# The third layer's modulation in a two-stage transformer kernel: scale and shift summed behind a bar, the gate formed on the tensor engine behind the experts

## The chip, the cores and the metric

The kernel runs on one core of one Trainium2 chip. The metric is the device time of one execution in microseconds (us); smaller is better. A core has a tensor engine (PE, with PEld for its weight loads), a vector engine (DVE), a scalar engine (ACT), GpSimd (POOL) and a sync engine (SP). Each takes its own instructions, and engines wait for each other by semaphores. Here SP's queue starts nearly all large transfers.

## The reference

Two blocks of two layers each work on 256 rows of width 1024 in f32. Each of the four layers has a mixer and a feed-forward part, and each part has a scale, a shift and a gate that come from a vector `c`:

```
def modulation(c, w, b):                       # first block; w is 1024 x 3072
    m = jnp.einsum("bd,de->be", jax.nn.silu(c), w) + b
    shift, scale, gate = jnp.split(m, 3, axis=-1)
...
# first block, layer 1 (the second of the four), feed-forward part
    logits = jnp.einsum("btd,de->bte", h, w_router).astype(jnp.float32)
    top_v, top_i = lax.top_k(logits, TOP_K)    # 2 of 8 experts for each row
...
# second block, layer 0 (the third of the four)
        mod = (cond @ w_mod[l] + b_mod[l])[:, None, :]
        sh_a, sc_a, g_a, sh_f, sc_f, g_f = jnp.split(mod, N_MOD, axis=-1)
        h = rms_norm_2(x, norm_mix[l]) * (1 + sc_a) + sh_a
...
        x = x + g_a * (jnp.concatenate([o_m, o_d], axis=-1) @ w_out[l])
```

## The kernel before

The work goes through eight steps: mixer and feed-forward part of each of four layers. Step 3 is the second layer's mixer, step 4 the router with eight experts, step 5 the attention of the third layer. Weights come in tiles of 1 MB into a pool `raw` of four buffers (two more, `rawx`, during the experts). Each is split by `split` into `hi` (a cast on ACT, line 159) and `lo` (a subtraction on DVE, line 160), and a product of f32 precision is three matmuls of these parts (lines 178 to 180; line 654 in the output projections).

A part's modulation is a product of a vector with a 1024x1024 block of weights. There are two ways to make it. `mod_rows` has DVE scale each of eight groups of 128 weight rows by its element of silu(c) and add it to an accumulator `macc` of 128x1024 (lines 318 and 320, two for each tile of 1 MB); `mod_done` then sums over the partitions on PE: eight products with one column each for a scale or a shift (`col`), two products of 128x512 for a gate. `mod_gate_pe` has PE do the whole: products of 128x512 with silu(c), broadcast to 128 columns, as the stationary part and the weight tile as the moving one, in plain f32, 16 for a gate and two more for its bias.

Which modulations are made beside which step is a table, `plan`. Before, step 4 begins with all three of the third layer's mixer, key (2, 0): scale, shift and gate by `mod_rows`. `LAG[4]` = 30 lowers their priority for the scheduler that puts each engine's instructions in order, and `self.bar` is None, so that they may also stand ahead of the end of step 3. `bar` is otherwise the last instruction of a norm's inverse root (line 220), and `behind` and `issue_after` keep work behind it.

The router part of step 4: `make_hf` transposes the normalised x of the second layer (`xn`) on PE, eight pairs through PSUM buffers of the pool `pp` (two buffers), and writes hf with scale and shift applied, on ACT and DVE in turn (lines 507 and 508). `route` multiplies by the router's weights (16 small products), copies the logits (line 1071) and forms the choice in small DVE steps (to line 1098, the selection `sel` at line 1082); a count goes to a register, and a branch on it follows. Then the experts run, and their results are gathered in four PSUM accumulators `ysum`. `resid_rms` makes the residual and two norms of it (lines 602 to 616), for which `two_rows` loads the gain and the shift of the post-norm into a `raw` buffer (line 479). Step 5 begins with the transposes of that result.

Of the kernel before, what the change touches and what calls it, by code (L numbers as in the profile page):

```python
# [14 lines left out]
ACT = mybir.ActivationFunctionType  # L15
ALU = mybir.AluOpType
# [4 lines left out]
KD = 8  # L21
# [46 lines left out]
class _Net:  # L68
# [210 lines left out]
    def mod_gate_pe(self, key):  # L279

        nc = self.nc
        w, b, j, c0 = self.mod_src(key)
        if self.modpos == 0:
            self.modacc = self.tl("gate", [128, D])
            nc.gpsimd.dma_start(out=self.modacc[0:1, :], in_=b[j * D:(j + 1) * D].unsqueeze(0))
        g = self.modacc
        h, k0 = self.modpos // 4, self.modpos % 4 * 2
        hs = slice(h * 512, (h + 1) * 512)
        if k0 == 0:
            self.modps = self.ps(pool="pa")  # L290
            self.mm(self.modps, self.ones[0:1, :], g[0:1, hs], True, False)
        wv = w.rearrange("(k p) n -> p k n", p=128)
        v = self.raw(wv[:, k0:k0 + 4, j * D + h * 512:j * D + (h + 1) * 512])
        for i in range(4):
            c = self.csil[:, c0 + k0 + i:c0 + k0 + i + 1]
            self.mm(self.modps, c.to_broadcast([128, 128]), v[:, i], False, k0 + i == KD - 1)
        if k0 == 4:
            self.plus(key, g[:, hs], self.modps)

    def mod_rows(self, key):  # L300

        nc = self.nc
        V = nc.vector
        w, b, j, c0 = self.mod_src(key)
        row = key[2] == "gate"
        if self.modpos == 0:
            self.modacc = self.tl("macc", [128, D])
            if row:
                nc.gpsimd.memset(self.modacc, 0.0)
                nc.gpsimd.dma_start(out=self.modacc[0:1, :], in_=b[j * D:(j + 1) * D].unsqueeze(0))  # L310
        acc = self.modacc
        wv = w.rearrange("(k p) n -> p k n", p=128)
        v = self.raw(wv[:, self.modpos:self.modpos + 2, j * D:(j + 1) * D])
        for i in range(2):
            k = self.modpos + i
            c = self.csil[:, c0 + k:c0 + k + 1]
            if k == 0 and not row:
                V.tensor_scalar(acc, v[:, i], c, None, ALU.mult)
            else:
                V.scalar_tensor_tensor(acc, v[:, i], c, acc, ALU.mult, ALU.add)  # L320

    def mod_done(self, key):

# [172 lines left out]
    def make_hf(self, xn, A, B):  # L496

        S, V = self.nc.scalar, self.nc.vector
        f = self.tl("h", [128, KD, T], tag="hh")
        for q in range(4):  # L500
            p = self.ps((128, 2, T))
            for t in range(2):
                for j in range(2):
                    k = 2 * q + j
                    self.tr(p[:, j, t * 128:(t + 1) * 128], xn[:, t, k * 128:(k + 1) * 128])
            k = 2 * q
            S.activation(f[:, k], p[:, 0], ACT.Identity, bias=B[:, k:k + 1], scale=A[:, k:k + 1])
            V.tensor_scalar(f[:, k + 1], p[:, 1], A[:, k + 1:k + 2], B[:, k + 1:k + 2], ALU.mult, ALU.add)
        return f

    def make_h(self, xn, A, B):
# [549 lines left out]
    def route(self, xn, hf):  # L1061
        nc, a = self.nc, self.a
        S, V, G = nc.scalar, nc.vector, nc.gpsimd
        wr = self.sc([128, KD, NE])
        G.dma_start(out=wr, in_=a["moe_router"][0].rearrange("(k p) e -> p k e", p=128))
        p = self.ps()
# [1 line left out]
            for k in range(KD):  # L1068
                self.mm(p[:, t * 8:t * 8 + 8], hf[:, k, t * 128:(t + 1) * 128], wr[:, k], k == 0, k == KD - 1)
        L = self.sc([128, 2, NE])  # L1070
        V.tensor_copy(L, p[:, 0:16].rearrange("p (t e) -> p t e", t=2))
        La = L[:, :, :, None].to_broadcast([128, 2, NE, NE])
        Lb = L[:, :, None, :].to_broadcast([128, 2, NE, NE])
        gt, eq = self.sc([128, 2, NE, NE]), self.sc([128, 2, NE, NE])
# [17 lines left out]
        p = self.ps()  # L1092
# [17 lines left out]
        p = self.ps()  # L1110
# [390 lines left out]
    def run(self):  # L1501
# [9 lines left out]
        SC, SH, GA = "scale", "shift", "gate"  # L1511
# [2 lines left out]
            1: [(0, 0, GA), (0, 1, SC), (0, 1, SH)],  # L1514
            2: [(0, 1, GA), (1, 0, SC), (1, 0, SH), (1, 0, GA), (1, 1, SC), (1, 1, SH)],
            3: [(1, 1, GA)],
            4: [(2, 0, SC), (2, 0, SH), (2, 0, GA)],
            5: [(2, 1, SC), (2, 1, SH)],
            6: [(2, 1, GA), (3, 0, SC), (3, 0, SH), (3, 0, GA), (3, 1, SC), (3, 1, SH)],
            8: [(3, 1, GA)],  # L1520
        }
        self.gates_pe = {(0, 0, GA)}
        LAG = {1: 100, 3: 100, 4: 30, 5: 30}
        FILL = {1: (4, 1, 1, 3, 1, 2), 2: (3, 2, 2), 3: (1, 1, 1, 1, 0, 0), 6: (2, 3), 8: (1, 0)}
        self.mods, self.modq, self.modpos = {}, [], 0
# [11 lines left out]
        for s in range(1, 9):  # L1537
            l, i = (s - 1) // 2, (s - 1) % 2
            self.step = s
            one = s < 5  # L1540
            if s == 2:
                self.later.append(self.rope_setup)
            with self.phase(**SIZES[s]):
                if one:
                    A, B = self.ab(l, i, g, b)
                else:
                    A, B = self.ab(l, i, self.c1("norm_ffn_2" if i else "norm_mix_2", l - 2))
                if s == 4:
                    self.bar = None
                    with self.phase(**ROUTE):  # L1550
                        self.mod_start(plan[4], LAG[4])
                        self.fill(KD * KD)
                        hf = self.make_hf(xn, A, B)
                        st = self.route(xn, hf)
                    with self.phase(**EXP):
                        order = self.granules()
                        ready = [self.raw(src) for src in order[:5]]
                        ready = [self.split(v) for v in ready[:2]] + ready[2:] + [self.raw(order[5])]
                        self.moe_over(st, A, B)
                        ysum = st[4]  # L1560
                        self.experts(0, *st[:4], A, B, ysum, order, True, ready)
                    get = lambda t, hh: ysum[t][hh]
                else:
                    h = self.make_h(xn, A, B)
                    self.mod_start(plan.get(s, []), LAG.get(s, 0))
                    if i == 0:
                        get = self.mixer(l, h, FILL[s]) if one else self.attn2(l - 2, h)
                    elif one:
                        get = self.ffn(h, a["ffn_w1"][0], a["ffn_w3"][0], a["ffn_w2"][0], FILL[s])
                    else:  # L1570
                        get = self.ffn(h, a["w_gate_2"][l - 2], a["w_up_2"][l - 2], a["w_down_2"][l - 2], FILL[s])
                rows = (a["post_ln_g"][l, i], a["post_ln_b"][l, i]) if one else None
                if s == 4:
                    x, xn = self.resid_rms(get, x, self.mod(l, i, "gate"), self.two_rows(*rows))
                else:
                    x, xn = self.resid(get, x, self.mod(l, i, "gate"), one, s < 8)
                if s < 4:
                    g, b = self.c1("post_ln_g", s - 1), self.c1("post_ln_b", s - 1)
                    x = xn
                    self.later.append(lambda x=x, r=rows: self.affine(x, *r))  # L1580
# [35 lines left out]
```

## Time and profile before

| what | value |
|---|---|
| median of 3 runs | 2067.67 us (2066.92 to 2073.77) |
| the profiled execution, its own time | 2068.1 us |
| its span in the trace | 2066.0 us |
| PE busy | 1926.2 us (93%) |
| DVE busy | 1643.8 us (80%) |
| ACT busy | 1208.2 us (58%) |
| HBM read | 552.19 MB |

Times within the trace count from the start of the span. A line of a profile names the source line, the engine, the operation, what it writes and reads (`out<-in`) and, in brackets, how long the engine had been idle before it and what let it go.

### The profile page before, as it was taken

To read this page: it belongs to the slowest core of one execution; us is meant where nothing else is said; L and a number is where in the kernel's file an instruction comes from. 1 tells how busy PE (TensorE), PEld (TensorE's weight loads), DVE (VectorE), ACT (ScalarE), POOL (GpSimd) and SP (SyncE) were. 2 spreads that over 40 slices of the span, in tenths; PEclk is the share of its full clock that TensorE was granted. 3 is DMA by queue.
4 is the path that set the end of the run, shared out by engine and by line. 5 is a ranking of instruction groups with operands and counts; after the bars stand their busy time and mean duration, and the time that the engine had idled before them with its cause. 6 is when DMAs were issued, how large, how long until landed. Compare 5 with 4: busy or idle time off the path is not lost.

```text
span 2066.0 us, 29939 instructions
## 1 busy us (share of the span) xinstructions
PE 1926.2 (93%) x11481; PEld 1660.4 (80%) x11481; DVE 1643.8 (80%) x2412; ACT 1208.2 (58%) x1817; POOL 50.2 (2%) x100
## 2 busy tenths in 40 slices
PE   3998999898499999999999999969989999998999
PEld 3887999886378787878778888858869998978998
DVE  6888987898598888888888888889778887667554
ACT  3455445562488767767776777755554546555442
POOL 4000000100000000000000000000000000000000
PEclk9999999998699999999999999979999999999999
DMA  9576999665399999899999999958339995326662
GB/s 325 184 276 214 348 329 316 195 223 205 144 330 362 339 332 341 319 357 346 345 326 350 348 355 358 364 187 279 138 119 349 335 328 164 123 86 220 204 204 82
DMA packets 283238, 555.25 MB, mean 269 GB/s; under 512 B 10172, under 2 KB 137520, under 8 KB 283088
## 3 DMA queue, kind: packets, MB, share of 16 engines
q1 hardware_dynamic: 280000, 549.49, 75.1%
q0 software_dynamic: 2656, 3.20, 0.9%
q8 instruction: 91, 1.49, 0.3%
q10 hardware_dynamic: 432, 0.58, 0.1%
q14 instruction: 59, 0.48, 0.1%
HBM read 552.19 MB, written 1.05 MB: 268 GB/s over the span
## 4 chain that ended last, share of the span: by engine, by line
PE 63%; DVE 6%; ACT 2%; issue 2%; DMA 0%; ACTq 0%; DVEq 0%
PE pp L179 11%; PE pp L180 11%; PE pp L178 11%; PE pa L654 6%; PE ya L179 4%; PE ya L178 4%; PE ya L180 4%; PE pp L187 3%; DVE lo L160 2%; PE pj L178 2%; PE pj L179 1%; PE pj L180 1%; PE sa L183 1%; PE pp L183 1%; ACT hi L159 1%
## 5 line engine op out<-in xcount | busy, mean ns | idle before, releaser
L160 DVE TENSOR_TENSOR lo<-raw,hi 128x1024 fp32r<-128x1024 f32 x660 | 786.0, 1219 | 177.3 <-ACT hi L159 168.6
L159 ACT CAST hi<-raw 128x1024 fp32r<-128x1024 f32 x660 | 667.4, 1050 | 344.2 <-PE pp L179 141.8
L178 PE MATMUL pp<-h,hi 128*128 128x256 f32 x960 | 270.7, 282 | 0.0
L180 PE MATMUL pp<-h,lo 128*128 128x256 f32 x960 | 267.8, 279 | 0.0
L179 PE MATMUL pp<-h,hi 128*128 128x256 f32 x960 | 267.7, 279 | 0.0
L160 DVE TENSOR_TENSOR lo<-rawx,hi 128x1024 fp32r<-128x1024 f32 x176 | 208.3, 1219 | 40.2 <-ACT hi L159 38.9
L320 DVE SCALAR_TENSOR_TENSOR macc<-raw,const,macc 128x1024 f32<-128x1024 f32 x168 | 215.2, 1281 | 9.9 <-DMA raw<-in_w_mod_dram 7.1
L180 PEld LDWEIGHTS pp<-h,lo 128*128 128x128 f32 x960 | 182.2, 190 | 0.1
L159 ACT CAST hi<-rawx 128x1024 fp32r<-128x1024 f32 x176 | 176.9, 1050 | 9.2 <-PE pp L180 7.4
L179 PEld LDWEIGHTS pp<-h,hi 128*128 128x128 f32 x960 | 180.6, 188 | 1.7 <-issue 1.2
L178 PEld LDWEIGHTS pp<-h,hi 128*128 128x128 f32 x960 | 180.3, 188 | 1.7 <-ACT hi L159 1.0
L179 PE MATMUL pp<-lo,h 128*128 128x512 f32 (+1 forms) x480 | 174.9, 365 | 1.3 <-DVE lo L160 1.0
L178 PE MATMUL pj<-hi,h 128*128 128x256 f32 x576 | 168.3, 293 | 7.2 <-ACT h L530 4.0
L178 PE MATMUL pp<-hi,h 128*128 128x512 f32 (+1 forms) x480 | 173.5, 362 | 0.2 <-ACT f L528 0.2
L179 PE MATMUL pj<-lo,h 128*128 128x256 f32 x576 | 165.1, 288 | 1.8 <-DVE lo L160 1.8
L180 PE MATMUL pj<-hi,h 128*128 128x256 f32 x576 | 164.8, 288 | 0.0
L654 PE MATMUL pa<-hi,s 128*128 128x512 f32 x528 | 148.2, 390 | 0.0
L179 PE MATMUL pp<-lo,xe 128*128 128x512 f32 (+1 forms) x384 | 144.9, 377 | 1.2 <-DVE lo L160 1.0
L180 PE MATMUL pp<-hi,x 128*128 128x512 f32 (+1 forms) x384 | 143.7, 374 | 0.0
L178 PE MATMUL pp<-hi,xe 128*128 128x512 f32 (+1 forms) x384 | 143.6, 374 | 0.0
L180 PE MATMUL pp<-hi,xe 128*128 128x512 f32 (+1 forms) x384 | 143.1, 373 | 0.0
L179 PE MATMUL ya<-lo,s 128*128 128x512 f32 x352 | 140.8, 400 | 0.0
(474 smaller groups left out, 3518.5 us busy)
## 6 DMA issues: line engine op xcount, KB each, us to landing
raw<-in_moe_w_dram SPq DMA_DIRECT2D x176, 1024.0 KB, 6.3
rawx<-in_moe_w_dram SPq DMA_DIRECT2D x88, 1024.0 KB, 6.3
raw<-in_ada_w_dram SPq DMA_DIRECT2D x48, 1024.0 KB, 6.7
raw<-in_w_mod_dram SPq DMA_DIRECT2D x48, 1024.0 KB, 6.9
raw<-in_w_in_dram SPq DMA_DIRECT2D x42, 1024.0 KB, 6.0
raw<-in_ffn_w_dram SPq DMA_DIRECT2D x33, 1024.0 KB, 6.3
raw<-in_w_gate_dram SPq DMA_DIRECT2D x22, 1024.0 KB, 5.2
raw<-in_w_up_dram SPq DMA_DIRECT2D x22, 1024.0 KB, 5.3
```

Source lines behind the costliest of these rows:

```text
L159: self.nc.scalar.copy(h, v[:, z:z + m])
L160: self.nc.vector.tensor_tensor(l, v[:, z:z + m], h.bitcast(F32), ALU.subtract)
L178: mm(out, lhsT=a[0], rhs=b[0], start=start, stop=False)
L179: mm(out, lhsT=a[0], rhs=b[1], start=False, stop=False)
L180: mm(out, lhsT=a[1], rhs=b[0], start=False, stop=stop)
L183: self.nc.tensor.matmul(out, lhsT=lhsT, rhs=rhs, start=start, stop=stop)
L187: self.nc.tensor.transpose(out, in_, self.ident[:p, :p])
L320: V.scalar_tensor_tensor(acc, v[:, i], c, acc, ALU.mult, ALU.add)
L654: mm(accs[t][h], lhsT=y[ia][:, s], rhs=W[ib][:, h * 512:(h + 1) * 512], start=start and ia == 0 and ib == 0, stop=stop and ia == 1)
```

## The change

The third layer's gate leaves the table's entry of step 4 and is made by `mod_gate_pe` after the experts, into a buffer of `pp`. Scale and shift lose their lag and are put behind `bar`, the end of the second mixer's norm. The logits' copy is put behind the last of their sums. `make_hf` writes all of hf on ACT.

```
@@ mod_gate_pe
-            self.modps = self.ps(pool="pa")
+            self.modps = self.ps(pool=self.gps)
@@ mod_rows
-                V.scalar_tensor_tensor(acc, v[:, i], c, acc, ALU.mult, ALU.add)
+                self.mod_last = V.scalar_tensor_tensor(acc, v[:, i], c, acc, ALU.mult, ALU.add)
@@ make_hf
-            V.tensor_scalar(f[:, k + 1], p[:, 1], A[:, k + 1:k + 2], B[:, k + 1:k + 2], ALU.mult, ALU.add)
+            S.activation(f[:, k + 1], p[:, 1], ACT.Identity, bias=B[:, k + 1:k + 2], scale=A[:, k + 1:k + 2])
@@ route
-        V.tensor_copy(L, p[:, 0:16].rearrange("p (t e) -> p t e", t=2))
+        with self.tc.issue_after(self.mod_last.ins):
+            V.tensor_copy(L, p[:, 0:16].rearrange("p (t e) -> p t e", t=2))
@@ run
-            4: [(2, 0, SC), (2, 0, SH), (2, 0, GA)],
+            4: [(2, 0, SC), (2, 0, SH)],
-        self.gates_pe = {(0, 0, GA)}
+        self.gates_pe = {(0, 0, GA), (2, 0, GA)}
+        self.gps = "pa"
-                    self.bar = None
                     with self.phase(**ROUTE):
-                        self.mod_start(plan[4], LAG[4])
-                        self.fill(KD * KD)
+                        self.mod_start(plan[4])
+                        with self.tc.issue_after(self.bar):
+                            self.fill(KD * KD)
+                        self.bar = None
                         hf = self.make_hf(xn, A, B)
                         st = self.route(xn, hf)
...
                     get = lambda t, hh: ysum[t][hh]
+
+                    self.gps = "pp"
+                    self.mod_start([(2, 0, GA)])
+                    self.fill(KD)
+                    self.gps = "pa"
```

On PE, between the last product of the second mixer and the first of the router, this stood before (`pp_5437` and `pp_5465` are the column sums of scale and shift, `pp_5495` and `pp_5498` the gate's two products, `x_5327` is xn, `pp_5532` the logits):

```order
L183 MATMUL pp_5437<-const_115,macc_5419 128x1 x8
L183 MATMUL pp_5465<-const_115,macc_5447 128x1 x8
...
L183 MATMUL pa_5583<-const_276 128x512
L183 MATMUL pp_5495<-macc_5475,const_115 128x512
L183 MATMUL pp_5498<-macc_5475,const_115 128x512
L187 MATMUL pp_5502<-const_113,x_5327 128x128 x4
L187 MATMUL pp_5509<-const_113,x_5327 128x128 x4
L187 MATMUL pp_5516<-const_113,x_5327 128x128 x4
L187 MATMUL pp_5523<-const_113,x_5327 128x128 x4
L183 MATMUL pp_5532<-sh_5530,h_5501 128x8 x16
```

And now:

```order
L183 MATMUL pa_5557<-const_276 128x512
L183 MATMUL pp_5437<-const_115,macc_5419 128x1 x8
L183 MATMUL pp_5465<-const_115,macc_5447 128x1 x8
L187 MATMUL pp_5476<-const_113,x_5327 128x128 x4
L187 MATMUL pp_5483<-const_113,x_5327 128x128 x4
L187 MATMUL pp_5490<-const_113,x_5327 128x128 x4
L187 MATMUL pp_5497<-const_113,x_5327 128x128 x4
L183 MATMUL pp_5506<-sh_5504,h_5475 128x8 x16
```

The gate's two products are gone, and the column sums of scale and shift stand directly ahead of the transposes.

On DVE, from the accumulators' end to the steps of the choice, this stood before (`macc_5475` is the gate's accumulator, `t_5549` the logits, `lo` the low parts of expert weights):

```order
L320 SCALAR_TENSOR_TENSOR macc_5475<-raw_5490,const_121,macc_5475 128x1024
L160 TENSOR_TENSOR lo_5628<-raw_5613,hi_5627 128x1024
...
L160 TENSOR_TENSOR lo_9694<-raw_5617,hi_9693 128x1024
L508 TENSOR_SCALAR h_5501<-pp_5502,col_5405,col_5407 128x256
L508 TENSOR_SCALAR h_5501<-pp_5509,col_5405,col_5407 128x256
L508 TENSOR_SCALAR h_5501<-pp_5516,col_5405,col_5407 128x256
L508 TENSOR_SCALAR h_5501<-pp_5523,col_5405,col_5407 128x256
L1071 COPY t_5549<-pp_5532 128x16
L1075 TENSOR_TENSOR sh_5551<-t_5549 128x128
L1076 TENSOR_TENSOR sh_5552<-t_5549 128x128
L1078 TENSOR_TENSOR sh_5552<-sh_5552,const_113 128x128
```

And now (`macc_5447` is the shift's accumulator, `t_5523` the logits):

```order
L320 SCALAR_TENSOR_TENSOR macc_5447<-raw_5460,const_121,macc_5447 128x1024 x2
L353 SCALAR_TENSOR_TENSOR col_5464<-pp_5465,const_272 128x8
L541 TENSOR_TENSOR col_16831<-col_5436,const_264 128x8
L160 TENSOR_TENSOR lo_5598<-raw_5587,hi_5597 128x1024
L160 TENSOR_TENSOR lo_5602<-raw_5587,hi_5601 128x1024
L1072 COPY t_5523<-pp_5506 128x16
L1076 TENSOR_TENSOR sh_5525<-t_5523 128x128
L1077 TENSOR_TENSOR sh_5526<-t_5523 128x128
L160 TENSOR_TENSOR lo_5606<-raw_5589,hi_5605 128x1024
L1079 TENSOR_TENSOR sh_5526<-sh_5526,const_113 128x128
L160 TENSOR_TENSOR lo_5610<-raw_5589,hi_5609 128x1024
L1080 TENSOR_TENSOR sh_5525<-sh_5525,sh_5526 128x128
```

All 16 sums of scale and shift now stand behind the inverse root's last step and end in the first row shown; two of the six splits stand ahead of the logits' copy and four between the steps behind it.

On SP's queue, at the end of the experts, the rows of the post-norm were followed by the attention's weights (`in_w_in`), and had directly behind them the last expert's weights:

```order
L131 DMA raw_16679<-in_moe_w_dram 128x2x1024
L479 DMA raw_16720<-in_post_ln_g_dram 128x1024
L479 DMA raw_16720<-in_post_ln_b_dram 128x1024
L131 DMA raw_16918<-in_w_in_dram 128x8x256
L131 DMA raw_16981<-in_w_in_dram 128x8x256
```

And now:

```order
L131 DMA raw_16653<-in_moe_w_dram 128x2x1024
L131 DMA raw_16698<-in_w_mod_dram 128x4x512
L131 DMA raw_16704<-in_w_mod_dram 128x4x512
L131 DMA raw_16713<-in_w_mod_dram 128x4x512
L131 DMA raw_16719<-in_w_mod_dram 128x4x512
L479 DMA raw_16726<-in_post_ln_g_dram 128x1024
L479 DMA raw_16726<-in_post_ln_b_dram 128x1024
L131 DMA raw_16924<-in_w_in_dram 128x8x256
L131 DMA raw_16987<-in_w_in_dram 128x8x256
```

The gate's four tiles stand between the last expert's weights and the rows of the post-norm, in the same four buffers.

## Rows read from the trace of the kernel before

**Rows 1.** Page, 40 slices of 51.65 us: PE's busy tenths and its granted clock.
```profile
PE   3998999898499999999999999969989999998999
PEclk9999999998699999999999999979999999999999
```

**Rows 2.** Timeline of PE around the router (start, duration, line, operation, idle before).
```profile
512.82 3.62 PE L183 MATMUL pp<-const,macc 128*128 128x1 f32 x32
...
531.72 3.55 PE L183 MATMUL pp<-macc,const 128*128 128x512 f32 x4 [14.39 <-DVE macc L320]
535.11 0.60 PE L187 MATMUL pp<-const,x 128*128 128x128 f32 x4
...
539.70 5.15 PE L183 MATMUL pp<-sh,h 128*128 128x8 f32 x32 [0.78 <-DVE h L508]
```

**Rows 3.** Stretches: length, busy PE, PEld, DVE, ACT, POOL, clock, DMA share, GB/s.
```profile
463.00:473.00 10.00, 6.35 (x22) 4.80 (x22) 6.78 (x13) 4.02 (x11) 0.00 (x0) 0.68 0.52 182
...
478.30:490.00 11.70, 10.49 (x43) 7.70 (x44) 8.66 (x32) 5.17 (x15) 0.90 (x1) 0.62 0.26 86
490.00:513.00 23.00, 23.00 (x108) 18.99 (x106) 19.66 (x29) 4.45 (x7) 0.00 (x0) 1.00 0.84 320
...
518.00:532.00 14.00, 0.28 (x1) 0.31 (x2) 13.93 (x15) 7.95 (x7) 0.00 (x0) 0.50 0.63 225
```

**Rows 4.** Timeline of ACT, at the router and behind the experts.
```profile
523.23 1.24 ACT L582 ACTIVATE x<-x,t,t 128x1024 f32<-128x1024 f32 x1 [25.64 <-DVE t L581]
...
538.50 1.02 ACT L507 ACTIVATE h<-pp,col,col 128x256 f32<-128x256 f32 x2 [1.29 <-PE pp L187]
...
1378.96 1.06 ACT L612 ACTIVATE x<-x 128x1024 f32<-128x1024 f32 x1
```

**Rows 5.** Timeline of DVE around the router.
```profile
523.04 0.15 DVE L581 SCALAR_TENSOR_TENSOR t<-t,t 128x1 f32<-128x1 f32 x1
523.16 3.93 DVE L320 SCALAR_TENSOR_TENSOR macc<-raw,const,macc 128x1024 f32<-128x1024 f32 x3
527.00 2.28 DVE L1103 TENSOR_TENSOR h<-x,x 128x2048 fp32r<-128x2048 f32 x1
...
531.54 5.76 DVE L160 TENSOR_TENSOR lo<-raw,hi 128x1024 fp32r<-128x1024 f32 x5
...
544.88 0.17 DVE L1071 COPY t<-pp 128x16 f32<-128x16 f32 x1 [4.78 <-PE pp L183]
...
546.59 0.17 DVE L1082 TENSOR_SCALAR t<-t 128x16 f32<-128x16 f32 x1
```

**Rows 6.** Waits from 463 to 565: who for whom, total us, times, longest.
```profile
PE pa L187 <- DVE P L943: 6.7, 2, 4.2
```

**Rows 7.** Timeline of DVE in the second mixer's softmax.
```profile
473.45 1.27 DVE L320 SCALAR_TENSOR_TENSOR macc<-raw,const,macc 128x1024 f32<-128x1024 f32 x1
```

**Rows 8.** Timeline of PE behind the experts.
```profile
1363.35 2.24 PE L183 MATMUL pa<-s,s 128*128 128x512 f32 x8 [0.33 <-ACT s L1261]
...
1383.73 1.97 PE L187 MATMUL pp<-const,x 128*128 128x128 f32 x8 [12.37 <-DVE x L615]
```

**Rows 9.** Groups by line and form: count, busy us, mean ns of one, idle before.
```profile
L159 ACT CAST hi<-raw 128x1024 fp32r<-128x1024 f32 x660 | 667.4, 1050 | 344.2 <-PE pp L179 141.8
...
L183 PE MATMUL pa<-raw,const 128*128 128x512 f32 x32 | 15.1, 601 | 0.0
...
L318 DVE TENSOR_SCALAR macc<-raw,const 128x1024 f32<-128x1024 f32 x16 | 12.0, 752 | 2.6 <-DMA raw<-in_ada_w_dram 1.4 <-DMA raw<-in_w_mod_dram 0.7 <-PE pa L183 0.4
```

**Rows 10.** Transfers issued from 1340 to 1400: count, KB each, median us to landing.
```profile
raw<-in_w_in_dram SPq DMA_DIRECT2D x5, 1024.0 KB, 5.2
...
raw<-in_post_ln_g_dram SPq DMA_DIRECT2D x1, 512.0 KB, 4.8
raw<-in_post_ln_b_dram SPq DMA_DIRECT2D x1, 512.0 KB, 6.6
```

**Rows 11.** Timeline of DVE in the norm behind the experts.
```profile
1372.19 1.27 DVE L608 SCALAR_TENSOR_TENSOR x<-x,t,raw 128x1024 f32<-128x1024 f32 x1
```

## The prediction

> **What bounds the kernel now.** I read the slices of the page first: TensorE (PE) is busy in nine tenths or more of most of them, with two holes, in the 11th and the 27th slice of 51.65 us, where the granted clock sinks too [rows 1]. Those two holes are the router and the seam between the experts and the third layer, and the change touches both. So I read each of them instruction by instruction.
>
> The router's hole: PE ends the column sums of the next layer at 516.4 (512.82 + 3.62) [rows 2], stands still in the stretch 518 to 532 at a clock of 0.50 [rows 3], and is let go at 531.72 by VectorE (DVE), after an idle of 14.39 us, for the two products that sum the gate's accumulator. Only behind them, at 535.11, come the transposes of xn [rows 2], although ScalarE (ACT) had the second half of xn ready at 523.23 + 1.24 = 524.5 [rows 4]. DVE has no gap there: up to 537.3 it does the steps of the inverse root, the eight sums of the gate, the low part of xn and six weight splits [rows 5]. DVE's queue sets the router's start, and PE's order hands it on: what waits first holds what stands behind.
>
> The mixer's end, before that: from 490 to 513 PE is busy all the time at full clock; between 463 and 490 it is not [rows 3], and 6.7 us of that, in two waits, is put down to DVE's probabilities P [rows 6]. In front of the second wait stand two sums of the third layer's scale, between DVE's maxima; one is shown [rows 7].
>
> The seam: PE's wait of 12.37 us up to 1383.73 is for the normalised x [rows 8], a pure chain of DVE and ACT. PE is free there, DVE and ACT are not.
>
> **The change part by part.** All times are on the clock of the profiled execution.
>
> *Sums that leave the mixer.* All 16 sums of scale and shift were done in or beside the mixer; now they wait for the bar, the last step of the inverse root. The two of [rows 7] stood in the chain of maxima, each for 1.2 us; without them P comes later only by ACT's exponentials, which I put at 1.5 us earlier than now. The lower bound of this is nothing, the upper the 6.7 us of [rows 6]. I take 1.5, because on both sides of 463 to 490 PE has no gap that DVE could close [rows 3].
>
> *Sums behind the bar.* Eight gate sums leave this place and 16 others come. The inverse root is no longer broken up: its result came at 523.04 with four sums between its steps, at 1.31 each (3.93 for three) [rows 5], so without them at 517.8, say 518.1 as the steps' own latency then shows. From there: 14 sums at 1.31 (18.3), two opening products at 0.75 (1.5) [rows 9], the low part of xn, 2.28 [rows 5]: 540.2. In between stands the first column, which DVE reads from eight products of PE with one column each. Sixteen such took 3.62 us [rows 2] at full clock, so eight take 1.8, and 3.6 if twice as slow; the router's 16 products in two levels took 5.15 [rows 2], so I take 2.7. DVE has one sum (1.3) to cover it and waits 1.4: 541.6. Less the mixer's 1.5: 540.1. Transfers are no bound: the second four tiles can each be issued when DVE has done with one of the first four, and a tile of 1 MB lands in 5.2 us [rows 10], before DVE comes to it.
>
> *The transposes behind the columns.* In PE's new order both column sums stand ahead of the transposes of xn, where before the gate's products did. So the transposes begin at 540.1 + 2.7 = 542.8 instead of 535.11: 7.7 later. This is what PE's order costs. The Trainium skill, "TensorE: Matmul & The Clock Gate", section "Step-by-step: what each phase is for", says that matmuls stay in program order and only weight loads are pulled ahead; the trace agrees: the transposes of [rows 2] came 10.6 us after x was ready (535.11 - 524.5). If matmuls could pass a waiting one, the sum would be that of the third rival below.
>
> *Evacuation on ACT alone.* Before, logits were read at 544.88, 9.8 after the transposes' start, with halves of hf written by DVE and ACT in turn. ACT writes one in 0.5 (1.02 for two) [rows 4]; now eight follow each other: 0.7 for the first transposes, then the third pair is out at 546.3 and the last at 547.2. The router's products take the third pair's buffer, so they run from 546.3 to 551.4 with their 5.15. Logits are read at 551.5: 6.6 later.
>
> *Splits within the choice.* Four of six weight splits, done before the transposes until now, stand between the small steps from the logits to the selection. They are ready, since their casts follow hf on ACT at once; each costs 1.15 (5.76 for five) [rows 5]: 4.6. Logits to selection was 1.7 (544.88 to 546.59) [rows 5]. From the selection on all is as before, and the experts' products, which fill PE afterwards, start later by 6.6 + 4.6 = 11.2. Nothing behind takes it back, since PE is full in the experts [rows 1]. Unknown is the clock of the products: 1 to 2 us on either side.
>
> *The gate at the seam.* 16 products of 128x512 in plain f32 and two of the bias. The first layer's gate made the same: 15.1 us for 16, 0.94 each [rows 9]; at the lower clock two took 3.55, 1.8 each [rows 2]. One bias product stands between the last expert's products and one product ahead of their gather into ysum, which until now waited 0.33 for ACT [rows 8]: 0.94 + 0.94 - 0.33 = 1.5 on the path. The gather ended at 1365.6 (1363.35 + 2.24) and now at 1367.1; the other 16 need 15.0 from there and end near 1382. The transposes come at 1386.4 (1383.73 + 2.7, below), so all 16 lie in PE's idle time before them. At 1.8 each they would end near 1396, 10 us too late; I take the full clock, as PE comes straight from dense work.
>
> The four 1 MB tiles stand on SP's queue ahead of the post-norm rows and of the next weights, and share their four buffers. The rows go out only when four gate products are done, near 1369.9 (1367.1 and three more at 0.94), and with 4.8 to landing [rows 10] come at 1374.7; DVE's first use, 1372.19 [rows 11], moves to about 1374.4. That is 0.3 late; 2 at worst if it takes the 6.6 of a loaded queue. One cast of the next weights (1.05 [rows 9]) now stands between ACT's two squares, the second of which started at 1378.96 [rows 4], and the root waits for it: 1.0. Together 1.5 + 0.2 + 1.0 = 2.7 at the seam, from nothing (all hidden) to 13.
>
> **Sum.** 11.2 + 2.7 = 13.9. The profiled execution took 2068.1 (span 2066.0), 0.4 above the median 2067.67. 2068.1 + 13.9 = 2082.0, by the median's measure 2081.6. A measurement can tell about 0.3%, 6.2 us, from no change.
>
> **The rivals.**
> 1. The seam loses its cover: the gate's products run at the lower clock or the rows and weights come late. For it: the clock fell in this very hole [rows 1]; against: it fell when PE stood still, and now PE works. 10 us more: 2092. Chance 0.10.
> 2. The mixer gives back more: both waits for P go (6.7) and with them the low clock of 463 to 473 and 478 to 490, where PE was busy 6.35 + 10.49 us [rows 3], half of which is 8.4. 15.1 instead of 1.5: 2068. Against: most of these gaps lie between PE and ACT, one after the other. Chance 0.12.
> 3. Waiting products don't hold the transposes. Then the logits are ready early, but DVE reads them behind all sums, the second column (542.8) and two splits (2.3): 545.1, 0.2 later than now, with the four splits 4.8, at the seam 2.7: 2075. [Rows 2] speak against it. Chance 0.06.
> 4. Faster: DVE was the mixer's bound, and the 16 sums stood on its path for 19.8 us (14 x 1.31 + 2 x 0.75), by which the mixer ends earlier; with the clock that comes back (8.4) up to 28. It decides from an end of the mixer 21.6 us earlier (13.9 + 1.5 + 6.2): 2055 to 2061. Against: PE busy 23.00 of 23.00 us from 490 to 513 [rows 3]. Chance 0.05.
>
> The forecast has 0.64, the remaining 0.03 is for what I don't see.
>
> **How the numbers follow.** The likeliest case alone spans 2076 to 2087 (columns at either clock, transfers, the mixer's gain from 0 to 4). To leave out no more than 2 in 10 the range reaches half-way into the second and nearly all of the first rival: 2071 to 2091. Slower holds the forecast, rivals 1 and 3 and a little: 0.81. Within 0.3%: rival 2 and the foot of the forecast, 0.13. Faster: rival 4 and the rest, 0.06.
>
> **What would show it.** After the mixer PE's wait for DVE's macc is about 22 us instead of 14.39, and its releaser is the last sum of the shift; the transposes start 7 to 8 us later; from logits to selection 6.3 us instead of 1.7, with four splits in it; the mixer's last product ends 1 to 2 us earlier. At the seam the gate's products show near 0.94 us at a clock of 1.0, and the first wait of the norm is the post-norm rows or nothing. The forecast is wrong if the first expert product comes less than 6 us later than now, if P's waits vanish together with the low clock, or if PE reaches the third layer's transposes after 1390 by the clock of before plus the router's loss.

## The result, and the profile after

The changed kernel takes 2083.52 us (median of 4 runs, 2082.59 to 2086.76), the kernel before in the same comparison 2068.81 (4 runs, 2066.92 to 2073.77): a ratio of 1.0071, 95% interval [1.0058, 1.0083]. It is slower, and inside the range. The profiled execution took 2083.43 with a span of 2081.7, so the spans differ by 15.7 and the medians by 14.7, where 13.9 was forecast.

The page of after, 40 slices: PE's busy tenths and its granted clock, to be laid beside [rows 1].

```profile
PE   3998999897499999999999999999989999998999
PEclk9999999997599999999999999999999999999999
```

The router's hole (10th and 11th slice) is a little deeper: PE's tenths go from 8 and 4 to 7 and 4, the clock's from 8 and 6 to 7 and 5. In the seam (27th slice) PE goes from 6 to 9 and the clock from 7 to 9.

PE's timeline of after around the router, beside [rows 2]:

```profile
531.44 3.57 PE L183 MATMUL pp<-const,macc 128*128 128x1 f32 x16 [18.27 <-DVE macc L320]
540.43 3.58 PE L183 MATMUL pp<-const,macc 128*128 128x1 f32 x16 [5.42 <-DVE macc L320]
543.87 1.95 PE L187 MATMUL pp<-const,x 128*128 128x128 f32 x8
546.07 2.03 PE L187 MATMUL pp<-const,x 128*128 128x128 f32 x8 [0.26 <-ACT h L508]
548.30 7.00 PE L183 MATMUL pp<-sh,h 128*128 128x8 f32 x32 [0.20 <-ACT h L508]
...
579.50 0.48 PE L178 MATMUL pp<-hi,xe 128*128 128x512 f32 x1
```

The two column sums wait 18.27 and 5.42 us for DVE's accumulators, and the transposes of xn stand behind them, at 543.87 instead of 535.11. The first expert product comes at 579.50; before, this was its line:

```profile
564.48 0.48 PE L178 MATMUL pp<-hi,xe 128*128 128x512 f32 x1
```

So the router loses 15.0.

DVE's timeline of after, beside [rows 5]:

```profile
535.13 5.24 DVE L320 SCALAR_TENSOR_TENSOR macc<-raw,const,macc 128x1024 f32<-128x1024 f32 x4
...
544.20 2.35 DVE L160 TENSOR_TENSOR lo<-raw,hi 128x1024 fp32r<-128x1024 f32 x2
555.33 0.18 DVE L1072 COPY t<-pp 128x16 f32<-128x16 f32 x1 [8.78 <-PE pp L183]
...
555.95 1.22 DVE L160 TENSOR_TENSOR lo<-raw,hi 128x1024 fp32r<-128x1024 f32 x1
...
561.17 0.17 DVE L1083 TENSOR_SCALAR t<-t 128x16 f32<-128x16 f32 x1
...
569.18 0.88 DVE L1153 TENSOR_SCALAR s<-const,t 128x128 fp32r<-128x128 f32 x4 [4.73 <-PEq L1124]
```

The last sum ends at 540.37. DVE then waits 8.78 us for the logits, does four splits (the first is shown) between the small steps of the choice, and has the selection at 561.17.

Two stretches of after (columns as in [rows 3]): PE's first wait, and the router's products.

```profile
518.00:532.00 14.00, 0.56 (x3) 0.56 (x3) 13.93 (x12) 2.63 (x2) 0.00 (x0) 0.50 0.71 253
...
548.30:555.30 7.00, 7.00 (x32) 6.90 (x32) 0.00 (x0) 4.63 (x6) 0.00 (x0) 0.50 0.37 137
```

All of it goes at the lower of the two levels of the clock: a granted 0.50.

The seam, PE's timeline of after, beside [rows 8]:

```profile
1380.18 2.49 PE L183 MATMUL pa<-s,s 128*128 128x512 f32 x8
1382.51 6.17 PE L183 MATMUL pp<-raw,const 128*128 128x512 f32 x14
...
1389.66 7.13 PE L183 MATMUL pp<-raw,const 128*128 128x512 f32 x16
...
1401.12 1.94 PE L187 MATMUL pp<-const,x 128*128 128x128 f32 x8 [3.68 <-DVE sh L1359]
...
1404.72 0.58 PE L178 MATMUL pj<-hi,h 128*128 128x256 f32 x1
...
1406.95 0.28 PE L179 MATMUL pj<-lo,h 128*128 128x256 f32 x1
```

The gate's products fill the idle time and end 4.3 us ahead of the transposes, which come 17.4 later than before: 15.0 from the router and 2.4 from the seam itself. From 1406.95 on a product takes 0.28 instead of 0.58 or 0.41, at a granted clock of 1.00 instead of 0.51. That is 2.2 us after the first projection; before, it came 4.5 after it (1387.30 to 1391.78).

ACT's timeline there, beside [rows 4], and the group of the gate's products, beside [rows 9]:

```profile
1395.32 1.03 ACT L159 CAST hi<-raw 128x1024 fp32r<-128x1024 f32 x1
1396.26 1.05 ACT L612 ACTIVATE x<-x 128x1024 f32<-128x1024 f32 x1
```

```profile
L183 PE MATMUL pp<-raw,const 128*128 128x512 f32 x32 | 14.3, 595 | 0.0
```

The cast stands between the two squares, as forecast, and a gate product costs 14.3 / 16 = 0.89. The clock in the stretch of these products was 1.00 (columns as in [rows 3]):

```profile
1382.51:1396.79 14.28, 14.28 (x34) 5.91 (x33) 12.61 (x26) 3.11 (x5) 0.00 (x0) 1.00 0.59 197
```

### The profile page after: what moved, and what is told of

Its sections match the earlier page's. It is cut to its first block, busy times and chain, and to the rows that moved or that the text cites. A ratio compares the mean times of both kernels' runs of the same rounds, so it can differ in the third digit from the quotient of the medians.

```text
span 2081.7 us, 29991 instructions
## 1 busy us (share of the span) xinstructions
PE 1943.2 (93%) x11513; PEld 1669.8 (80%) x11513; DVE 1632.7 (78%) x2400; ACT 1209.1 (58%) x1821; POOL 49.6 (2%) x99
## 4 chain that ended last, share of the span: by engine, by line
PE 61%; DVE 6%; ACT 3%; issue 2%; DMA 1%; ACTq 0%; DVEq 0%
PE pp L179 11%; PE pp L180 11%; PE pp L178 11%; PE pa L654 6%; PE ya L179 4%; PE ya L178 4%; PE ya L180 4%; PE pp L187 2%; DVE lo L160 2%; PE pj L178 1%; PE pj L180 1%; PE pj L179 1%; PE pp L183 1%; PE sa L183 1%; ACT hi L159 1%
## 5 line engine op out<-in xcount | busy, mean ns | idle before, releaser
L320 DVE SCALAR_TENSOR_TENSOR macc<-raw,const,macc 128x1024 f32<-128x1024 f32 x160 | 204.8, 1282 | 16.5 <-DMA raw<-in_w_mod_dram 8.8
```

Source lines behind the costliest of these rows:

```text
L320: self.mod_last = V.scalar_tensor_tensor(acc, v[:, i], c, acc, ALU.mult, ALU.add)
```

## The experiments

The theory on trial: DVE's sums hold PE's column sums, PE's order hands that on to the transposes, DVE's order hands the splits on to the branch; the gate's move costs 2 to 3 at the seam. Rivals: the evacuation on ACT is what costs; the clock is what costs; the gate's move costs more than it shows. The times in the columns two to four are starts in the timelines of the profiled executions. Each ratio is against runs of the kernel before made beside it on the same chip (medians from 2068.61 to 2069.46). Differences of 2 to 4 us between two changed kernels are read from the traces first: there the intervals of the ratios often overlap.

| kernel | logits read | first expert product | third layer's transposes | span | median (runs) | ratio [95%] |
|---|---|---|---|---|---|---|
| before | 544.88 | 564.48 | 1383.73 | 2066.0 | 2068.81 (4) | |
| after | 555.33 | 579.50 | 1401.12 | 2081.7 | 2083.52 (4) | 1.0071 [1.0058, 1.0083] |
| cols_last | 537.58 | 568.46 | 1392.07 | 2071.8 | 2075.58 (7) | 1.0031 [1.0019, 1.0042] |
| cols_late | 537.26 | 562.71 | 1388.74 | 2073.4 | 2073.75 (11) | 1.0018 [1.0009, 1.0027] |
| cols_late2 | 537.35 | 561.71 | 1384.19 | 2069.2 | 2070.11 (11) | 1.0002 [0.9993, 1.0011] |
| choice_first | 552.32 | 576.76 | 1397.73 | 2080.7 | 2085.70 (5) | 1.0081 [1.0068, 1.0095] |
| splits_first | 553.86 | 574.84 | 1396.45 | 2076.6 | 2079.43 (5) | 1.0061 [1.0048, 1.0075] |
| evac_both | 557.93 | 578.82 | 1401.68 | 2085.4 | 2085.30 (5) | 1.0078 [1.0064, 1.0092] |
| warm | 552.48 | 576.37 | 1397.21 | 2078.4 | 2084.49 (5) | 1.0080 [1.0066, 1.0094] |
| no_gate | 554.67 | 578.57 | 1398.27 | 2080.2 | 2080.87 (5) | 1.0055 [1.0041, 1.0069] |
| gate_only | 534.62 | 555.85 | 1376.94 | 2058.3 | 2060.04 (5) | 0.9954 [0.9940, 0.9967] |
| gate_evac | 536.62 | 557.66 | 1378.73 | 2061.4 | 2062.34 (7) | 0.9974 [0.9963, 0.9985] |
| gate_zeros | 535.00 | 555.92 | 1377.23 | 2059.6 | 2059.89 (5) | 0.9949 [0.9935, 0.9962] |
| gate_tidy | 532.47 | 554.16 | 1376.86 | 2063.1 | 2060.06 (5) | 0.9949 [0.9936, 0.9963] |

**cols_last.** The edit keeps the accumulators and forms both columns after `route`:

```
-                    self.mods[key] = self.mod_done(key)
+                    if self.defer is None:
+                        self.mods[key] = self.mod_done(key)
+                    else:
+                        self.defer.append((key, self.modacc))
...
                         st = self.route(xn, hf)
+                        for key, self.modacc in self.defer:
+                            self.mods[key] = self.mod_done(key)
```

> The changed kernel with both column sums of scale and shift put behind the router's products in PE's order; the sums themselves still stand ahead of the logits' copy on DVE. If PE's order is what holds the transposes, they start when xn is ready, near 520 instead of 543.87, and the logits are read when DVE's last sum ends, near 540.5 instead of 555.33; with one or two splits left in the choice the router gives back 14 to 16 us: 2068 to 2070. If the transposes wait for something else (xn itself, a free buffer), they stay near 543 and the time stays within 2 us of the changed kernel, 2083.5. If PE's order holds them but DVE is the bound behind it, the gain is only the column sums, the evacuation and the router's products, about 9: 2074.

PE's and DVE's timelines of cols_last:

```profile
514.25 0.66 PE L187 MATMUL pp<-const,x 128*128 128x128 f32 x4 [1.29 <-DVE x L589]
518.57 1.12 PE L187 MATMUL pp<-const,x 128*128 128x128 f32 x4 [3.67 <-ACT x L585]
...
523.65 7.00 PE L183 MATMUL pp<-sh,h 128*128 128x8 f32 x32 [0.20 <-ACT h L511]
...
544.62 6.97 PE L183 MATMUL pp<-const,macc 128*128 128x1 f32 x32
```

```profile
537.58 0.17 DVE L1075 COPY t<-pp 128x16 f32<-128x16 f32 x1
...
548.21 0.17 DVE L356 SCALAR_TENSOR_TENSOR col<-pp,const 128x8 f32<-128x8 f32 x1 [3.01 <-PE pp L183]
...
551.63 0.17 DVE L356 SCALAR_TENSOR_TENSOR col<-pp,const 128x8 f32<-128x8 f32 x1 [3.17 <-PE pp L183]
```

The transposes start at 514.25 (x's first half) and the logits are read right behind the last sum: 17.75 earlier. Sixteen products with one column each, moved behind the transposes and the router's products, did that. They took their two PSUM buffers with them, so this run alone doesn't tell PE's order from a wait for a buffer. The trace of after does: there DVE had read the first column by 535.2 (535.05 + 0.17), which frees one of the two buffers, and x was ready, yet the transposes came at 543.87, behind the second column's products. Not all came back: the column sums now stand ahead of PE's branch, and DVE waits for both (3.01 and 3.17) ahead of its own.

**cols_late, cols_late2.** The column sums go behind the experts; in the second, DVE's reads of them go behind the norm's root as well.

```
                     self.fill(KD)
                     self.gps = "pa"
+                    for key, self.modacc in later:
+                        self.mods[key] = self.mod_done(key)
```

```
                     x, xn = self.resid_rms(get, x, self.mod(l, i, "gate"), self.two_rows(*rows))
+                    with self.behind():
+                        for key, self.modacc in later:
+                            self.mods[key] = self.mod_done(key)
```

> The changed kernel with the column sums of scale and shift formed behind the experts, after the gate's products; the 16 sums on DVE and everything else stay as in the changed kernel. In the run with the column sums behind the router's products, ahead of PE's branch, the logits were read at 537.58, but DVE still waited for both column sums (3.01 and 3.17) before its branch, and the time was 2075.6. If PE's order of the column sums is what costs, now 6 to 8 more come back: 2068 to 2070, level with the kernel before. If the 14 to 16 us of DVE's sums ahead of the logits are a cost of their own that the order only hid, it stays near 2073 to 2075. If the column sums delay the third layer's start, it ends between.

> The run with the column sums behind the experts (2073.75), with DVE's two reads of them put behind the root of the second norm there, in place of ahead of it. In that run DVE stood in these reads for 3.08 and 2.04 us with the root behind them in its queue, and from DVE's L614 to L618 it took 10.71 us where the changed kernel took 7.28 for the same steps. If that is the seam's loss, 3 come back: 2070 to 2071, level with the kernel before by 0.1%. If the reads only wait elsewhere (the transposes' evacuation needs them), it stays at 2073 to 2074.

DVE's timelines at the seam, first of cols_late, then of cols_late2:

```profile
1382.69 0.17 DVE L356 SCALAR_TENSOR_TENSOR col<-pp,const 128x8 f32<-128x8 f32 x1 [3.08 <-PE pp L183]
1384.90 0.17 DVE L356 SCALAR_TENSOR_TENSOR col<-pp,const 128x8 f32<-128x8 f32 x1 [2.04 <-PE pp L183]
```

```profile
1382.21 0.16 DVE L356 SCALAR_TENSOR_TENSOR col<-pp,const 128x8 f32<-128x8 f32 x1
...
1383.96 0.17 DVE L356 SCALAR_TENSOR_TENSOR col<-pp,const 128x8 f32<-128x8 f32 x1 [0.89 <-PE pp L183]
```

In cols_late the router is 1.8 better than before, but DVE stands in the two reads for 5.1 us with the root behind them, and from PE's gather (1364.37) to the transposes it takes 24.4 instead of the 20.9 of after (1380.18 to 1401.12). With the reads behind the root it is 20.9 again (1363.30 to 1384.19), and the median falls by 3.6 as expected. 13.4 of the 14.7 that the change cost are gone, by the place of two column sums and of their reads; what is left (ratio 1.0002, interval 0.9993 to 1.0011) can't be told from nothing.

**choice_first, splits_first.** Both move weight splits out of the choice: the first puts four behind the selection, the second puts all six ahead of the logits' copy.

```
-                        ready = [self.split(v) for v in ready[:2]] + ready[2:] + ...
+                        one, self.bar = self.split(ready[0]), self.chosen
+                        ready = [one] + [self.split(v) for v in ready[1:3]] + ready[3:] + ...
```

```
-        with self.tc.issue_after(self.mod_last.ins):
+        with self.tc.issue_after(self.lo_last.ins):
             V.tensor_copy(L, ...)
...
+                        order = self.granules(); early = [self.split(self.raw(src)) for src in order[:3]]; self.nraw += 3
                         st = self.route(xn, hf)
```

> The changed kernel with four of the six weight splits put behind the selection on DVE, where DVE waits 4.73 us for PE's branch. If these splits are what makes the choice 5.84 us long, logits to selection falls to about 1.7 and the router gives back 4: 2079.5. If they only move and the branch or the first expert's products then wait for them, the first expert product comes as late as in the changed kernel and the time stays at 2083.5.

> The changed kernel with the logits' copy put behind all six weight splits on DVE instead of behind the last sum, so that the splits stand where DVE waits 8.78 us for PE's router products. If the four splits lie on the path because DVE must end them ahead of its branch, logits to selection falls from 5.84 to 1.7 and the first expert product comes 4 earlier: 2079.5 against 2083.5. In the run with the splits behind the selection the choice was 1.7 long and nothing was gained. If the casts on ACT, which follow hf, come too late for this, the logits are copied later by what the choice gets shorter: 2083.5.

DVE's timelines, first of choice_first, then of splits_first (L1072 the logits' copy, L1083 the selection, L1153 the first step behind the branch):

```profile
552.32 0.17 DVE L1072 COPY t<-pp 128x16 f32<-128x16 f32 x1 [6.28 <-PE pp L183]
...
554.03 0.17 DVE L1083 TENSOR_SCALAR t<-t 128x16 f32<-128x16 f32 x1
554.12 1.22 DVE L160 TENSOR_TENSOR lo<-raw,hi 128x1024 fp32r<-128x1024 f32 x1
...
566.31 0.88 DVE L1153 TENSOR_SCALAR s<-const,t 128x128 fp32r<-128x128 f32 x4 [5.50 <-DVEq L1124]
```

```profile
548.64 4.63 DVE L160 TENSOR_TENSOR lo<-raw,hi 128x1024 fp32r<-128x1024 f32 x4 [3.56 <-ACT hi L159]
553.86 0.17 DVE L1072 COPY t<-pp 128x16 f32<-128x16 f32 x1 [0.58 <-PE pp L183]
...
555.56 0.17 DVE L1083 TENSOR_SCALAR t<-t 128x16 f32<-128x16 f32 x1
...
563.40 0.87 DVE L1153 TENSOR_SCALAR s<-const,t 128x128 fp32r<-128x128 f32 x4 [4.55 <-PEq L1124]
```

The choice is 1.7 long in both. From the logits to the step behind the branch it is 13.99 in choice_first, as in after (13.85), since the splits still stand ahead of DVE's branch; in splits_first it is 9.54, since four of them ran while PE made the logits. Its median is 4.1 below that of after, as much as the term, though the intervals of the two ratios overlap. That of choice_first is 2.2 above, no clear difference either: its logits were read 3.0 earlier, but 2.5 of that is another matter, since its router's products happened to run at a higher clock (shown further down).

**evac_both.** `make_hf` as in the kernel before.

```
-            S.activation(f[:, k + 1], p[:, 1], ACT.Identity, bias=..., scale=...)
+            V.tensor_scalar(f[:, k + 1], p[:, 1], A[:, k + 1:k + 2], B[:, k + 1:k + 2], ALU.mult, ALU.add)
```

> The changed kernel with hf written by ACT and DVE in turn again, as in the kernel before; the scheduler then also moves most of the weight splits ahead of the logits' copy. If ACT alone is what makes the evacuation long, the router's products start 0.5 to 1 earlier than 4.43 after the transposes' start; with the choice at about 2.9 instead of 5.84 the time is 2079 to 2080. If the splits, which now stand between DVE's writes of hf, wait for their casts on ACT, hf comes later and the time is 2084 to 2088.

DVE's timeline of evac_both:

```profile
547.12 0.99 DVE L508 TENSOR_SCALAR h<-pp,col,col 128x256 f32<-128x256 f32 x2
548.03 2.36 DVE L160 TENSOR_TENSOR lo<-raw,hi 128x1024 fp32r<-128x1024 f32 x2
550.30 0.99 DVE L508 TENSOR_SCALAR h<-pp,col,col 128x256 f32<-128x256 f32 x2
```

Two splits stand between DVE's writes of hf, and the router's products start 6.4 after the transposes (544.51 to 550.90) instead of 4.4. So ACT alone is the shorter way to the logits. The first expert product comes no later (578.82 against 579.50), as more splits now lie ahead of the logits' copy, and the medians can't be told apart. The evacuation is not where the time went.

**warm.** Products of zeros keep PE busy in both waits.

```
+    def spin(self):
+        dm, dp, n = self.dummy
+        for _ in range(n):
+            self.mm(dp[0:8, :]..., dm, self.maskb[:, None, 128:256].to_broadcast([128, 4, 128]))
```

> The changed kernel with 72 products of bf16 zeros on PE, whose results nobody reads: 46 from the end of the root on, ahead of the first column sum, and 26 between the two column sums. They fill PE's two waits of 18.27 and 5.42 us. If the column sums (3.57 and 3.58), the transposes (3.98) and the router's products (7.00) are slow because PE comes to them at the lower clock, the column sums take 1.8, the transposes about 2 and the products 3.5 to 4.5, and the router gives back 2 x 1.8 + 2 + 2.5 to 3.5, 8 to 9 of it on the path: 2074.5 to 2076. If these durations belong to the shapes and not to the clock, nothing comes back, or the zeros delay the first column sum: 2083 to 2088.

PE's timeline of warm:

```profile
517.72 12.78 PE L183 MATMUL ya<-const,t 128*8 128x512 bf16 x46 [4.35 <-DVE t L1562]
531.63 1.95 PE L183 MATMUL pp<-const,macc 128*128 128x1 f32 x16 [1.12 <-DVE t L1562]
...
540.85 1.95 PE L183 MATMUL pp<-const,macc 128*128 128x1 f32 x16
...
546.22 6.22 PE L183 MATMUL pp<-sh,h 128*128 128x8 f32 x32 [0.25 <-ACT h L513]
```

The column sums fall from 3.57 to 1.95, with the granted clock at 0.96 and 1.00 instead of 0.50: that was the clock, not the shape. The router's products fall to 6.22 only, at 0.57. In the profiled execution the first expert product comes 3.1 earlier, and that execution (2080.13) is 3.3 below that of after. But it is the fastest of five; the others took 2082.95 to 2085.78, and the median shows nothing of the 8 to 9 expected. So the trace confirms the term, and a remedy isn't shown.

**no_gate.** The third layer's gate is left out; the second layer's stands in its place, so the output is another.

```
-                    self.mod_start([(2, 0, GA)])
-                    self.fill(KD)
+                    self.mods[(2, 0, GA)] = self.mods[(1, 1, GA)]
```

> The changed kernel without the third layer's gate: its 18 products, its four tiles and its bias are left out, and the second layer's gate is used in its place, so the output is another. What remains against the kernel before is the router alone. By the prediction's sum the seam costs 2.7: 2080.8. By the trace of the changed kernel the seam loses 2.4 up to the transposes and gets 2.1 back by a clock that rises sooner, so leaving the gate out gains 0.3 only: 2083.2. If the gate's loads cost the experts anything, more than 4 comes back: below 2079.5.

From the first expert product to the third layer's transposes it is 819.70, as before (819.25), against 821.62 in after. The median is 2.65 lower, with overlapping intervals. By trace and median the seam costs some 2 to 2.7. Whether the clock that rises sooner at 1406.95 gives anything back stays open: behind the transposes after is 1.35 shorter than no_gate (680.58 and 681.93), less than these kernels scatter there.

**gate_only, gate_evac, gate_zeros, gate_tidy.** Scale and shift go back beside the mixer; the gate stays behind the experts.

```
-                        self.mod_start(plan[4])
-                        with self.tc.issue_after(self.bar):
-                            self.fill(KD * KD)
-                        self.bar = None
+                        bar, self.bar = self.bar, None
+                        self.mod_start(plan[4], LAG[4])
+                        self.fill(KD * KD)
+                        self.bar = bar
```

gate_evac also has evac_both's edit. gate_zeros adds four rounds of zeros behind `ysum`'s opening products in `route`; gate_tidy moves splits and a cast with `issue_after`.

```
+        for _ in range(4):
+            for t in range(2):
+                for h in range(2):
+                    self.mm(ysum[t][h]..., self.maskb[:, 128:256], ..., False, False)
```

> The changed kernel with scale and shift summed beside the mixer again, as in the kernel before; the gate stays on PE behind the experts, and make_hf stays on ACT. If DVE's eight gate sums and the two products that waited for them were what held the router before, the transposes start near 521 instead of 535.11, the first expert product comes 12 to 14 us earlier than in the kernel before, and with 1 to 3 lost at the seam the time is 2055 to 2058. If the experts' first weights don't come earlier, half of it: 2062. If the router was bound by something other than the gate's sums, only the seam's loss is left: 2069 to 2071.

> Scale and shift summed beside the mixer as in the kernel before, the gate on PE behind the experts as in the changed one, and hf written by ACT and DVE in turn as before: only the gate's move is left of the change. With ACT alone this kernel measured 2060.04. If two engines write hf faster, its products start 1 earlier: 2059. If the splits between DVE's writes hold hf up: 2060 to 2063. Either way it stays 5 us or more below the kernel before, since the eight gate sums are gone from the router.

> The kernel with scale and shift beside the mixer and the gate behind the experts (2060.04), with 16 more bf16 products of zeros added into the experts' accumulators, which change no value; they stand between the mixer's last product and the transposes, where PE waits. If the lower clock is what makes the router's products 7.00 long, they take 3.5 to 5 and the time falls by 2 to 4: 2056 to 2058. In the run with 72 zeros the profiled execution was 3.3 shorter and the median was not; if that holds, it stays at 2059 to 2061.

> The kernel with scale and shift beside the mixer and the gate behind the experts (2060.04), with two things tidied: the weight splits on DVE stand behind the step that lets ACT finish xn (L581) and ahead of the logits' copy, and ACT's cast of the next weights stands behind both squares of the norm at the seam, not between them. One split of 1.15 stood ahead of L581, one cast of 1.03 between the squares. If both lie on the path, 2 come back: 2058. If the transposes or the router's products hide the first, 1: 2059. No change, 2060, if neither is on the path.

gate_only is 8.6 faster than the kernel before: its first expert product comes 8.6 earlier, and from there to the third layer's transposes it takes 1.8 longer (821.09 against 819.25). The gain expected was 11 to 13; 1.4 of it goes to a later end of the mixer (the mixer's last product ends at 514.38 instead of 512.98) and 1.9 to the router's products (7.00 at the lower clock). gate_evac, where hf is written as before, loses 2.3 against it in the median and 1.8 at the first expert product. gate_zeros and gate_tidy change nothing in the median. In gate_zeros the clock was 1.00 while the zeros ran (518.48 to 523.90), and still the router's products took 7.00 at 0.50 from 527.96 on. gate_tidy's profiled execution shows the first expert product 1.7 earlier and the seam 0.8 shorter, but it was its slowest (2064.88; the fastest 2057.03), so whether the tidying is worth 1 or 2 stays open.

## Why the prediction was right, step by step

- **Sums that leave the mixer** (1.5 earlier): the mixer's last product ends at 511.37 instead of 512.98, 1.6 earlier (the first line is of before, the second of after):

```profile
512.59 0.39 PE L654 MATMUL pa<-hi,h 128*128 128x512 f32 x1
```

```profile
510.98 0.39 PE L654 MATMUL pa<-hi,h 128*128 128x512 f32 x1
```

 PE's waits for P are shorter by 1.8 and still there (beside [rows 6]):

```profile
PE pa L187 <- DVE P L943: 4.9, 2, 2.6
```

 So rivals 2 and 4 fall. With the sums back beside the mixer it ends later again, at 514.38 in gate_only.
- **Sums behind the bar** (end at 540.1): 540.37, in part by luck: DVE waited 2.47 us for the first column, not 1.4, and the 14 sums took 0.8 less than 18.3.
- **The transposes behind the columns** (542.8, 7.7 later): 543.87, 8.8 later. Each column sum took 3.57, not 2.7; the upper bound of that term was the right one. cols_last shows the mechanism, and rival 3 (waiting products don't hold the transposes) falls with it.
- **Evacuation on ACT alone** (logits read 6.6 later): 10.45 later. This is the mis-sized term: 1.1 from the later transposes (0.9 of it the column sum), 0.9 from the evacuation (the products start 4.4 after the transposes, not 3.5, as ACT had to wait for the second half of them), 1.9 from the router's products, which took 7.00 and not the 5.15 of [rows 2]. The prediction took a duration that before had at a mixed clock. The stretches of these products, in before, after and choice_first, show three clocks for the same 32 records:

```profile
539.70:544.90 5.20, 5.14 (x32) 5.05 (x32) 0.42 (x2) 0.00 (x0) 0.00 (x0) 0.70 0.84 324
```

```profile
547.80:552.30 4.50, 4.48 (x32) 4.39 (x32) 0.00 (x0) 4.50 (x6) 0.00 (x0) 0.81 0.59 218
```

 They took 5.14 at a granted 0.70, 7.00 at 0.50 (shown above) and 4.48 at 0.81. The length of the waits ahead of them doesn't sort these: choice_first had the same two waits as after (18.27 and 5.42), and in gate_only, with waits of 3.34 and 2.10, they took 7.00. What sets the clock there stays open.
- **Splits within the choice** (4.6): 5.84 - 1.71 = 4.1 in the trace, and splits_first's median agrees. The size is right; from the selection on it was not quite as before, as the step behind the branch came 0.4 later still (5.2 instead of 4.7 after the cast of the count). choice_first shows that it is the branch, not the selection, that the splits hold up.
- **The gate at the seam** (2.7): 2.4 in the trace against before, 1.9 against no_gate (2.65 by the medians). Of the 2.4, 1.4 are there at DVE's first residual step (1364.93 before, 1381.31 in after, less the router's 15.0), and 0.8 come between DVE's L611 (1376.45 and 1392.95) and ACT's second square (1378.96 and 1396.26), where the cast stands. The post-norm rows cost next to nothing (from the first residual step to L611 it is 11.52 before and 11.64 in after). Their term had a slip: 1372.19 and the 1.5 on the path make 1373.7, not 1374.4, and the sum then took 0.2 where the text has 0.3. Rival 1 falls: the products kept the upper clock (1.00, shown above).
- **The sum**: 11.2 + 2.7 was 15.0 (10.45, 4.1 and 0.4) + 2.4. Behind the transposes the spans come 1.7 closer (680.58 us to the end, 682.27 before). The other kernels scatter from 679.73 to 686.24 there, so that 1.7 is scatter as far as these runs tell, and it made the forecast look better than its router term was.

What the forecast did not ask is which half of the change was worth having. The gate's move gains 8.6 with hf on ACT (gate_only) and 6.3 with hf as before (gate_evac); the sums' move with its column sums ahead of the transposes turned that into a loss of 14.7. From gate_only to after it is 23.5, and the columns' place is 13.4 of it: with the columns out of the way cols_late2 is still 10.1 above gate_only. Of these 10.1 the traces show 5.9 at the first expert product: the logits, copied behind the last of the sums, are read 2.7 later, and from there it takes 3.1 longer, with splits between the steps of the choice again. The other 4 are 1.4 up to the third layer's transposes and scatter behind them.

## What to carry to other kernels

Sixteen products of 0.45 us each (3.57 / 8) cost 13 us because they stood, waiting, ahead of work that was ready: ask of each small step in an in-order queue what waits behind it, and when it is moved, move its reader with it. Work that hides behind an engine's wait is free only if it ends ahead of the next thing in that engine's own queue that others wait for, a branch included. Price small products between waits at the lower clock first, and not at what one execution at a mixed clock showed: eleven of the fourteen profiled executions here had the router's products at 7.0.

## What the runs showed of the hardware

- The same products of the router took 4.48 to 7.00 us in different executions, with the granted clock between 0.81 and 0.50; in twelve kernels out of fourteen the profiled execution had them at 6.2 to 7.0.
- The column sums, 16 records each, took 3.57 at a granted 0.50 (after) and 1.95 at 0.96 and 1.00 (warm).
- One kernel is granted different clocks in different executions. Of eleven executions of the kernel before, made beside splits_first, the fastest took 2064.83 at a mean granted clock of 0.974 and the slowest 2072.47 at 0.967. The five of gate_tidy lie between 2057.03 and 2064.88, at 0.973 to 0.975, so the clock isn't all of it. The time of a single execution says little about differences below 8 us.
- From DVE's cast of the count, on which the branch goes, to its first step behind the branch it takes 4.7 before (549.45 to 554.17) and 5.2 after (564.02 to 569.18) with small steps only in between, 8.3 in choice_first (558.04 to 566.31) with two splits in between, and 6.7 in cols_late2 (544.55 to 551.25) with three. So the branch's own latency hid part of the splits in one kernel and none in the other; why is open.
